# RWKV-7 chunk inverses on 32-wide diagonal tiles, with the decays' affine steps folded away and the normed rows completed later

## The chip, the cores and the metric

The kernel runs on one core of a Trainium2 chip. The metric is device time in microseconds (us), from start to end of one launch. Engines are called as in the profile: PE (TensorE matmul), PEld (its weight load), DVE (VectorE), ACT (ScalarE), POOL (GpSimd), SP (SyncE, which issues most DMAs).

## What is computed

The reference is a whole small network on 256 tokens of width 1024, in float32. A first block of two attention and feed-forward layers ends in an RMS norm. A second block of two layers follows: a layer norm, a hybrid mixer, a residual and layer norm, a mixture of 32 experts, a residual and layer norm. The hybrid mixer has three parts side by side, on one input projection: SSD (512 wide), RWKV-7 (256 wide, 4 heads of 64) and GLA (256 wide). The change touches RWKV-7, whose recurrence per head is

```
w = -softplus(-(w0 + tanh(w_lr) @ w2)) - 0.5;  decay = exp(-exp(w));  a = sigmoid(a0 + a_lr @ a2)
k = k * (1 + (a - 1) * k_a)
sa    = state @ (-kk_t)
state = state * w_t + sa (kk_t * a_t)^T + v_t k_t^T
y_t   = state @ r_t
```

## The kernel before

The kernel does not run the recurrence step by step. It cuts the 256 tokens into two chunks of 128 (NT = 2, index c). Inside a chunk, all `sa` follow from a unit-triangular system of 128 x 128 per head; the kernel forms its inverse `Ti` (4 heads side by side, 128 x 512) and multiplies with it (L1083). Each layer l of the second block calls `ln_T` (norm and transpose of the rows), `mixer` and `moe`, in this order.

**Norm.** `ln_T` leaves the rows `x` centred but not yet scaled. Its inner function `finish` completes them, x = x * r + bias row, with two ACT operations (L791) and two POOL operations (L792) of 128 x 1024. They are needed only at the residual, at the mixer's end. The mixer calls `finish` right after the low-rank projections (L918).

**Decays and rates.** The low-rank projections give `ld` and `av` as a tanh (ACT, L920). Two DVE operations (L931, L932) turn them into log decays and rates with a multiply and an add. Prefix sums over time follow (L937), then `rel` and `ex` (L945, L947), their exponentials (L948 to L950), and `bet`, `alp` (L963 to L966), the factors of the pair matrices (`pairmat`, L981).

**Inverse.** From the pair matrix in PSUM, DVE makes `N` (L994), and `Ti` starts as the part of N next to the diagonal, plus the identity (L995, L996); PE transposes it into `X` (L999). Then six levels double the size of the inverted diagonal blocks. Per level and chunk:

```
M  = N * mask of the level      POOL L1004, 128 x 512
pw = M^T X     (4 heads)        PE L1007, then ACT copy Wm, L1009
px = Ti^T Wm   (levels 1 to 5)  PE L1013, then DVE X += px, L1018
pt = Wm^T Ti                    PE L1016, then DVE Ti += pt, L1019
```

All are full 128 x 128 matrices, though at level lv only blocks of 2^lv are nonzero in what is added. A float32 matmul of this kind has two records in the trace, so one group of 4 heads is 8 records.

**Order.** A scheduler in the framework decides the order on each engine when the program is built; on the chip every engine runs its list in order. Between the groups of the inverse it places whatever else is ready: the projections (helpers at L129, fp32 weights split into two parts by ACT L159 and DVE L161), the other pair matrices (L981), and the block on `w_small` (L1134 to L1165: dt, the GLA gates and their scan). After the inverse come the RWKV output (L1078 to L1120), the rest of the `gv` and `gg` projections (L129), the GLA score matmuls (L1212, 32 x 32 tiles given by `tile_position`), SSD, the out-projection, and the experts. The experts' weights are asked for once a tile of the GLA output exists.

## Time and profile before

| what | us |
|---|---|
| median of 3 runs (1994.29 to 1998.39) | 1995.66 |
| profiled execution, total | 1999.68 |
| its span in the trace | 1998.0 |
| PE busy | 1861.1 (93%) |
| DVE busy | 784.9 (39%) |
| ACT busy | 600.1 (30%) |
| POOL busy | 194.6 (10%) |

The profiled execution's granted TensorE clock is 0.973 on average. The page's slices of 49.95 us show the stages: the first block up to about 606 us, the mixer of layer 0 in slices 13 to 17, its experts up to about 1300 us, the mixer of layer 1 in slices 27 to 31, its experts up to the end. A busy share is an average over all of these, so the mixers have to be read by windows of their own.

### The profile page before, as it was taken

What the parts mean: (1) busy time and instruction counts of PE and PEld (TensorE: products, weight loads), DVE (VectorE), ACT (ScalarE), POOL (GpSimd) and SP (SyncE); (2) the same over time, 40 slices, a digit from 0 to 9 for tenths busy, and PEclk for the clock granted to TensorE, in tenths of its full rate; (3) what the DMA queues carried; (4) which work ended last, traced back from release to release, by engine and by line L of the source; (5) the groups of instructions that cost most, each with busy time, mean ns of one, the idle gap of its engine ahead of it and who ended that gap; (6) DMA issues with size and microseconds to landing.
All of it is one profiled execution on the core that took longest, in us unless ns stands there. A gap on an engine that the chain in (4) does not pass through costs nothing. (4 is left out here: it accounts for less than half of the span.)

```text
span 1998.0 us, 28881 instructions
## 1 busy us (share of the span) xinstructions
PE 1861.1 (93%) x11910; PEld 1285.7 (64%) x11910; DVE 784.9 (39%) x1401; ACT 600.1 (30%) x1002; POOL 194.6 (10%) x321
## 2 busy tenths in 40 slices
PE   8999999999998899899999999879999999999996
PEld 7889998889997788644444333378886444443333
DVE  5654445754447867511111011078574111111012
ACT  5554444654445434211111011153442111111011
POOL 1100000100012423200000000034231000000000
PEclk9899999999999999899999999989998999999998
DMA  6245553345562116699999999841277999999995
GB/s 243 103 154 186 188 198 127 106 158 184 186 251 99 64 65 274 244 385 419 417 418 419 418 418 419 341 141 43 86 295 259 413 418 418 418 418 419 418 418 213
DMA packets 90494, 542.49 MB, mean 272 GB/s; under 512 B 10416, under 2 KB 10928, under 8 KB 38128
## 3 DMA queue, kind: packets, MB, share of 16 engines
q1 hardware_dynamic: 87552, 531.21, 67.8%
q0 software_dynamic: 2512, 9.16, 1.3%
...
HBM read 539.43 MB, written 1.05 MB: 271 GB/s over the span
## 5 line engine op out<-in xcount | busy, mean ns | idle before, releaser
L161 DVE TENSOR_TENSOR hl<-w,hl 128x1024 fp32r<-128x1024 f32 (+2 forms) x252 | 300.2, 1200 | 237.9 <-ACT hl L159 235.4
L159 ACT ACTIVATE hl<-w 128x1024 fp32r<-128x1024 f32 (+2 forms) x252 | 256.6, 1027 | 292.6 <-PE aux L129 113.1
L1726 PE MATMUL aux<-ew_e,XG_e 128*64 128x512 f32 x992 | 253.5, 595 | 7.6 <-DMA ew_e<-in_moe_up 7.5
L1736 DVE SCALAR_TENSOR_TENSOR e_sh_e<-e_sh_e,e_kept_e,aux 128x512 f32<-128x512 f32 x32 | 23.9, 747 | 509.4 <-ACT e_sh_e L1735 496.8
L1726 PEld LDWEIGHTS aux<-ew_e,XG_e 128*64 128x64 f32 x992 | 81.9, 137 | 165.5 <-issue 148.4
L1745 ACT ACTIVATE e_sh_e<-m 128x512 f32<-128x512 f32 x32 | 19.1, 598 | 508.9 <-PE m L1743 508.9
L1726 PE MATMUL aux<-hl,XG_e 128*64 128x512 f32 x480 | 137.8, 606 | 10.1 <-DMA hl<-in_moe_up 6.2
L129 PE MATMUL aux<-hl_f,hl 128*128 128x256 f32 x1056 | 131.4, 284 | 0.6 <-DVE hl_f L245 0.3
L129 PEld LDWEIGHTS aux<-hl_f,hl 128*128 128x128 f32 x1056 | 129.7, 192 | 2.8 <-DVE hl_f L245 0.7
L1726 PE MATMUL aux<-w,XG_e 128*64 128x512 f32 x384 | 126.7, 594 | 5.1 <-DMA w<-in_moe_gate 5.1
L129 PE MATMUL m<-hl_f,hl 128*128 128x256 f32 x1056 | 130.3, 283 | 0.0
L129 PEld LDWEIGHTS m<-hl_f,hl 128*128 128x128 f32 x1056 | 128.3, 192 | 0.0
L1758 DVE TENSOR_TENSOR e_y_e<-m,e_y_e 128x512 fp32r<-128x512 f32 x64 | 44.2, 691 | 213.3 <-ACT e_y_e L1757 213.3
L182 PE MATMUL mm<-hl,m_f 128*128 128x512 f32 x528 | 123.5, 390 | 0.0
L1754 PE MATMUL m<-ew_e,e_sh_e 128*64 128x512 f32 x448 | 115.5, 597 | 0.0
L182 PEld LDWEIGHTS mm<-hl,m_f 128*128 128x128 f32 x528 | 97.9, 188 | 19.4
L1757 ACT ACTIVATE e_y_e<-m 128x512 fp32r<-128x512 f32 x64 | 38.2, 597 | 199.8 <-PE m L1754 199.8
L1726 PEld LDWEIGHTS aux<-hl,XG_e 128*64 128x64 f32 x480 | 41.9, 138 | 82.3 <-issue 52.3
L1650 PE MATMUL m<-e_y_e,e_h_e 128*128 128x256 f32 x256 | 69.2, 308 | 24.1 <-DVE e_y_e L1636 24.1
L129 PE MATMUL aux<-hl_m,hl 128*128 128x256 f32 (+1 forms) x576 | 83.3, 305 | 6.5 <-DVE r_k_m L898 4.9
L1766 PE MATMUL mm<-e_y_e,slots_e 128*128 128x512 f32 x256 | 78.4, 429 | 6.1 <-PEq L1789 4.7
L129 PEld LDWEIGHTS aux<-hl_m,hl 128*128 128x128 f32 (+1 forms) x576 | 77.0, 200 | 9.4 <-DVE r_k_m L898 5.1
(560 smaller groups left out, 2850.2 us busy)
## 6 DMA issues: line engine op xcount, KB each, us to landing
...
```

Source lines behind the costliest of these rows:

```text
L129: self.nc.tensor.matmul(out, x, y, start=(i == 0 and j == 0), stop=(i == n - 1 and j == len(terms) - 1))
L159: nc.scalar.activation(vo(hv), s, AF.Copy)
L161: nc.vector.tensor_tensor(vo(lv), s, vo(hv).bitcast(F32), op=OP.subtract)
L182: self.nc.tensor.matmul(acc[t][h], u1, u2, start=(kg == 0 and q == 0), stop=(kg == n_k - 1 and q == len(terms) - 1))
L1650: nc.tensor.matmul(p[:, j], src[:, t, c], sel[t], start=n == 0, stop=n == 3)
L1726: nc.tensor.matmul(p[64 * i:64 * i + 64], xg[:, 4 * q + kk, o:o + CAP], tiles[nm, q, e](kk), start=(q == 0 and kk == 0), stop=(q == 1 and ...
L1736: i = nc.vector.scalar_tensor_tensor(s_, s_, at[pr][1], up, op0=OP.mult, op1=OP.mult)
L1745: nc.scalar.activation(hh, p, AF.Copy)
L1754: nc.tensor.matmul(p[64 * i:64 * i + 64], hh[:, f, 64 * i:64 * i + 64], tiles["down", hf, es[i]](f), start=f == 0, stop=f == 3)
L1757: nc.scalar.activation(yh, p, AF.Copy)
L1758: nc.vector.tensor_tensor(yl, p, yh.bitcast(F32), op=OP.subtract)
L1766: nc.tensor.matmul(acc[t][hf], sT[:, t * P:(t + 1) * P], ys[:, 2 * hf + q], start=False, stop=pr == last and q == 1)
```

## The change

Four things change in `mixer` and `ln_T`.

1. The inverse works on the four 32 x 32 diagonal blocks of each head for levels 1 to 4, as 32 x 32 matmuls with `tile_position` (32b, 32b); `TX` holds a 32-wide `Ti` and its transpose, which DVE's 32 x 32 block transpose makes from the sum (no `px` step, no PE transposes). One POOL operation per chunk makes all four masked copies `Ml`. Level 5 joins pairs of blocks (32 x 32 tiles off the diagonal), level 6 the two halves (64 x 64 tiles). Ti is zeroed by POOL and filled by copies. The masks lv0 to lv6 are gone, and with them 896 columns of the constants' load.
2. The affine steps on `ld` and `av` are gone; their constants go into the scan, the exponentials' scale and two fused operations.
3. `finish` is four DVE operations of 128 x 512, issued after the last copy of the inverse.
4. The block on `w_small` stands ahead of the inverse in the program.

```diff
-MCONST = (("blk", P), ("gla_mask", 192)) + tuple((f"lv{n}", P) for n in range(7))
+MCONST = (("blk", P), ("gla_mask", 192))
-    early = T([P, 2048], "x_early")
+    early = T([P, 1088], "x_early")
@@ ln_T
     def finish(after):
-        r2 = k.t(W, [P, NT], "ln_r2")
-        for t in range(NT):
-            nc.gpsimd.tensor_copy(r2[:, t:t + 1], after)
-            nc.gpsimd.tensor_copy(r2[:, t:t + 1], rs[t])
-            nc.scalar.activation(x[:, t], x[:, t], AF.Copy, scale=r2[:, t:t + 1])
-            nc.gpsimd.tensor_tensor(x[:, t], x[:, t], rows[1], op=OP.add)
+        for xh, r, h in ((xh, rs[t], h) for t in range(NT) for h, xh in enumerate(row_halves(x)[t])):
+            with k.tc.issue_after(after):
+                nc.vector.scalar_tensor_tensor(xh, xh, r, rows[1][:, h * 512:(h + 1) * 512], op0=OP.mult, op1=OP.add)
 
@@ mixer: decays and rates
-    finish(lr[:, :1])
...
     cd = -0.5 * math.exp(-0.5)
-    nc.vector.tensor_scalar(ld, ld, cd, cd, op0=OP.mult, op1=OP.add)
-    nc.vector.tensor_scalar(av, av, 0.5, 0.5, op0=OP.mult, op1=OP.add)
-
     cum = T([P, 2, S], "r_cum")
     for j in range(2):
         for c in range(NT):
-            nc.vector.tensor_tensor_scan(cum[:, j, tk(c)], k.ones, ld[:, j, tk(c)], 0.0, op0=OP.mult, op1=OP.add)
+            nc.vector.tensor_tensor_scan(cum[:, j, tk(c)], k.ones, ld[:, j, tk(c)], 0.0, op0=OP.add, op1=OP.add)
     cv = cum.rearrange("p j (c t) -> p j c t", c=NT)
     mid, last = cv[:, :, :, 63], cv[:, :, :, P - 1]
     nc.vector.tensor_sub(car, last[:, :, 0], mid[:, :, 0])
     nc.vector.tensor_add(car, car, mid[:, :, 1])
-    nc.scalar.activation(car, car, AF.Exp)
+    nc.scalar.activation(car, car, AF.Exp, scale=cd)
     rel, ex, e_in = (T([P, 2, S], f"r_{n}") for n in ("rel", "ex", "ein"))
     nc.vector.tensor_tensor(rel.rearrange("p j (c t) -> p j c t", c=NT), cv,
                             mid[:, :, :, None].to_broadcast([P, 2, NT, P]), op=OP.subtract)
-    nc.vector.tensor_sub(ex, rel, ld)
-    nc.scalar.activation(e_in, rel, AF.Exp, scale=-1.0)
-    nc.scalar.activation(ex, ex, AF.Exp)
-    nc.scalar.activation(rel, rel, AF.Exp)
+    nc.vector.scalar_tensor_tensor(ex, rel, -1.0, ld, op0=OP.add, op1=OP.subtract)
+    nc.scalar.activation(e_in, rel, AF.Exp, scale=-cd)
+    nc.scalar.activation(ex, ex, AF.Exp, scale=cd)
+    nc.scalar.activation(rel, rel, AF.Exp, scale=cd)
...
     bet = T([P, 2, S], "r_bet")
-    nc.vector.tensor_mul(bet, av, kk_)
-    nc.vector.tensor_mul(bet, bet, e_in)
+    nc.vector.scalar_tensor_tensor(bet, av, 1.0, kk_, op0=OP.add, op1=OP.mult)
+    nc.vector.scalar_tensor_tensor(bet, bet, 0.5, e_in, op0=OP.mult, op1=OP.mult)
...
@@ mixer: the inverses (the block on w_small, dt and the gate scan now stands ahead of this)
+    lvm = const["gla_mask"]
+    Ti = [T([P, 4, P], f"r_T{c}") for c in range(NT)]
+    blk = lambda b: slice(32 * b, 32 * b + 32)
+    up, dn = slice(0, 64), slice(64, P)
+    TX, Ml, M5, M6, X6 = {}, {}, {}, {}, {}
     for c in range(NT):
+        nc.gpsimd.memset(k.late(Ti[c], anchor=r2[:, 0, :1]), 0.0)
+        f1, f2 = (T([P, 512], f"r_{n}{c}") for n in "XN")
+        h4 = lambda x: x.rearrange("p (h t) -> p h t", h=4)
+        X6[c], M5[c], N, M6[c] = h4(f1[:64, :256]), h4(f1[:, 256:384]), h4(f1[:, 384:]), h4(f2[:64, :256])
+        TX[c] = f2[:, 256:].rearrange("p (i h t) -> p i h t", i=2, h=4)
+        nc.gpsimd.memset(k.late(X6[c][blk(0), :, 32:], anchor=r2[:, 0, :1]), 0.0)
         p = pairmat(bet, alz, c)
-        N[c], X[c], Ti[c] = (T([P, 4, P], f"r_{n}{c}") for n in "NXT")
-        nc.vector.tensor_tensor(N[c], p, b4(r2[:, c]), op=OP.mult)
-        nc.vector.tensor_tensor(Ti[c], N[c], mask("lv0"), op=OP.mult)
-        nc.vector.tensor_tensor(Ti[c], Ti[c], k.ident[:, None, :].to_broadcast([P, 4, P]), op=OP.add)
-        p = k.ps([P, 4, P])
+        for b in range(4):
+            nc.vector.tensor_tensor(N[blk(b)], p[blk(b), :, blk(b)], b4(r2[:, c], 32)[blk(b)], op=OP.mult)
+        Ml[c] = T([P, 4, 4, 32], f"r_M{c}")
+        nc.gpsimd.tensor_tensor(Ml[c], N[:, None].to_broadcast([P, 4, 4, 32]),
+                                lvm[:, :4, None].to_broadcast([P, 4, 4, 32]), op=OP.mult)
+        nc.vector.tensor_tensor(TX[c][:, 0], N, lvm[:, 4:5].to_broadcast([P, 4, 32]), op=OP.mult)
+        nc.vector.tensor_tensor(TX[c][:, 0], TX[c][:, 0], lvm[:, 5:6].to_broadcast([P, 4, 32]), op=OP.add)
+        nc.vector.transpose(TX[c][:, 1].rearrange("p h t -> p (h t)"), TX[c][:, 0].rearrange("p h t -> p (h t)"))
+        for b in (0, 2):
+            nc.vector.tensor_tensor(M5[c][blk(b)], p[blk(b), :, blk(b + 1)], b4(r2[:, c], 32)[blk(b)], op=OP.mult)
+        nc.vector.tensor_tensor(M6[c], p[up, :, dn], b4(r2[:, c], 64)[up], op=OP.mult)
+    def tiles32(out, lhs, rhs, rows, cols):
         for h_ in range(4):
-            nc.tensor.transpose(p[:, h_], Ti[c][:, h_], k.ident)
-        nc.scalar.activation(X[c], p, AF.Copy)
-    for lv in range(1, 7):
+            for b, q in zip(rows, cols):
+                nc.tensor.matmul(out[blk(q), h_], lhs(b, h_), rhs(b, h_), start=True, stop=True,
+                                 tile_position=(32 * b, 32 * q))
+    for lv in range(1, 5):
         for c in range(NT):
-            M = T([P, 4, P], "r_M", bufs=4)
-            nc.gpsimd.tensor_tensor(M, N[c], mask(f"lv{lv}"), op=OP.mult)
-            pw = k.ps([P, 4, P])
-            for h_ in range(4):
-                nc.tensor.matmul(pw[:, h_], M[:, h_], X[c][:, h_], start=True, stop=True)
-            Wm = T([P, 4, P], "r_W", bufs=2)
+            t_, x_, M = TX[c][:, 0], TX[c][:, 1], Ml[c][:, 4 - lv]
+            pw = k.ps([P, 4, 32])
+            tiles32(pw, lambda b, h_: M[blk(b), h_], lambda b, h_: x_[blk(b), h_], range(4), range(4))
+            Wm = T([P, 4, 32], "r_W", bufs=2)
             nc.scalar.activation(Wm, pw, AF.Copy)
-            if lv < 6:
-                px = k.ps([P, 4, P])
-                for h_ in range(4):
-                    nc.tensor.matmul(px[:, h_], Ti[c][:, h_], Wm[:, h_], start=True, stop=True)
-            pt = k.ps([P, 4, P])
-            for h_ in range(4):
-                nc.tensor.matmul(pt[:, h_], Wm[:, h_], Ti[c][:, h_], start=True, stop=True)
-            if lv < 6:
-                nc.vector.tensor_add(X[c], X[c], px)
-            nc.vector.tensor_add(Ti[c], Ti[c], pt)
+            p = k.ps([P, 4, 32])
+            tiles32(p, lambda b, h_: Wm[blk(b), h_], lambda b, h_: t_[blk(b), h_], range(4), range(4))
+            nc.vector.tensor_add(t_, t_, p)
+            nc.vector.transpose(x_.rearrange("p h t -> p (h t)"), t_.rearrange("p h t -> p (h t)"))
+    for c in range(NT):
+        for b in (1, 3, 0, 2):
+            nc.scalar.activation(Ti[c][blk(b), :, blk(b)], TX[c][blk(b), 0], AF.Copy)
+        for b in (0, 1):
+            nc.gpsimd.tensor_copy(X6[c][blk(b), :, blk(b)], TX[c][blk(b), 1])
+        t5 = lambda b, h_: TX[c][blk(b), 0, h_]
+        pw = k.ps([P, 4, 32])
+        tiles32(pw, lambda b, h_: M5[c][blk(b), h_], lambda b, h_: TX[c][blk(b), 1, h_], (0, 2), (1, 3))
+        Wm = T([P, 4, 32], "r_W", bufs=2)
+        for b in (1, 3):
+            nc.scalar.activation(Wm[blk(b)], pw[blk(b)], AF.Copy)
+        p = k.ps([P, 2, 4, 32])
+        w5 = lambda b, h_: Wm[blk(b), h_]
+        tiles32(p[:, 1], t5, w5, (1,), (1,))
+        tiles32(p[:, 0], w5, t5, (1, 3), (0, 2))
+        nc.vector.tensor_copy(X6[c][blk(1), :, blk(0)], p[blk(1), 1])
+        nc.scalar.activation(Ti[c][blk(2), :, blk(3)], p[blk(2), 0], AF.Copy)
+        nc.vector.tensor_copy(Ti[c][blk(0), :, blk(1)], p[blk(0), 0])
+    for c in range(NT):
+        pw = k.ps([P, 4, 64])
+        for h_ in range(4):
+            nc.tensor.matmul(pw[dn, h_], M6[c][:, h_], X6[c][:, h_], start=True, stop=True, tile_position=(0, 64))
+        Wm = T([P, 4, 64], "r_W6", bufs=2)
+        nc.scalar.activation(Wm[dn], pw[dn], AF.Copy)
+        p = k.ps([P, 4, 64])
+        for h_ in range(4):
+            nc.tensor.matmul(p[up, h_], Wm[dn, h_], Ti[c][dn, h_, dn], start=True, stop=True, tile_position=(64, 0))
+        i = nc.vector.tensor_copy(Ti[c][up, :, dn], p[up])
+    finish(i.ins)
...
-        nc.vector.tensor_scalar(f, av[:, j], col("k_a", j), oka[:, j:j + 1], op0=OP.mult, op1=OP.add)
+        nc.vector.tensor_scalar(f, av[:, j], hka[:, j:j + 1], oka[:, j:j + 1], op0=OP.mult, op1=OP.add)
```

What this does to the lists shows at three places, all in layer 0. On PE, in the middle of the inverse (`mm` are the inverse's results in PSUM, r_T, r_X, r_W its operands, `m3` other results), before:

```order
L1016 MATMUL mm_534_5981<-r_T0_m0_513_5900,r_W_m0_532_5974 128x128 x4
L1007 MATMUL mm_536_5990<-r_X1_m0_517_5914,r_M_m0_535_5988 128x128 x4
L129 MATMUL m3_601_6246<-r_bs_m0_580_6171,x_early_m0_475_5547 128x512
L1013 MATMUL mm_538_5997<-r_W_m0_537_5995,r_T1_m0_518_5915 128x128 x4
L1016 MATMUL mm_539_6002<-r_T1_m0_518_5915,r_W_m0_537_5995 128x128 x4
L1007 MATMUL mm_541_6011<-r_X0_m0_512_5899,r_M_m0_540_6009 128x128 x4
```

and now, where r_N0 and r_N1 hold TX of the two chunks:

```order
L1052 MATMUL mm_530_6055<-r_N0_m0_517_5940,r_M0_m0_519_5950 32x32 x16
L1131 MATMUL m3_568_6410<-r_rows_m0_563_6396,r_AK0_m0_567_6408 128x64 x3
L977 MATMUL m3_569_6416<-r_alz0_m0_490_5654,r_k_m0_500_5686 128x256
L1052 MATMUL mm_532_6074<-r_N0_m0_517_5940,r_W_m0_531_6072 32x32 x16
L1052 MATMUL mm_533_6093<-r_N1_m0_521_5961,r_M1_m0_523_5971 32x32 x16
L977 MATMUL m3_569_6416<-r_alz1_m0_491_5657,r_k_m0_500_5686 128x256
L1052 MATMUL mm_535_6112<-r_N1_m0_521_5961,r_W_m0_534_6110 32x32 x16
```

Three groups of four full matmuls per level and chunk became two groups of sixteen small ones, with less other work between them.

On DVE, at the decays, before:

```order
L161 TENSOR_TENSOR hl_68<-w_67,hl_68 128x320
L931 TENSOR_SCALAR r_ld_m_484_5633<-r_ld_m_484_5633 128x512
L932 TENSOR_SCALAR r_av_m_485_5634<-r_av_m_485_5634 128x512
L937 SCALAR_TENSOR_TENSOR r_cum_m_496_5678<-const_69,r_ld_m_484_5633 128x128 x4
L941 TENSOR_TENSOR x_small_m_476_5548<-r_cum_m_496_5678 128x2
```

and now (L933 is the scan, L896 a token shift of k):

```order
L896 SCALAR_TENSOR_TENSOR r_k_m_500_5686<-aux_5695,const_69,r_k_m_500_5686 128x255
L161 TENSOR_TENSOR hl_68<-w_67,hl_68 128x320
L896 SCALAR_TENSOR_TENSOR r_k_m_500_5686<-aux_5695,const_69,r_k_m_500_5686 128x255
L933 SCALAR_TENSOR_TENSOR r_cum_m_495_5669<-const_69,r_ld_m_484_5635 128x128 x2
L1100 TENSOR_SCALAR r_f_m_560_6381<-r_av_m_485_5636,x_small_m_476_5548 128x256
L1101 TENSOR_TENSOR r_k_m_500_5686<-r_k_m_500_5686,r_f_m_560_6381 128x256
```

The two operations between the tanh and the scan are gone, and both halves of k's token shift stand ahead of the scan.

On DVE, at the end of the inverse, now:

```order
L1084 COPY r_T1_m0_515_5936<-mm_553_6335 32x4x32
L1095 COPY r_T0_m0_514_5935<-mm_556_6358 64x4x64
L1140 SCALAR_TENSOR_TENSOR r_QB1_m0_580_6452<-m3_579_6449,x_small_m0_476_5548 128x128
L1144 TENSOR_TENSOR r_QK1_m0_582_6460<-m3_581_6457,x_small_m0_476_5548 128x512
L1095 COPY r_T1_m0_515_5936<-mm_559_6371 64x4x64
L789 SCALAR_TENSOR_TENSOR x_1_64<-x_1_64,ln_st_m0_457_5475,row_n_456_5472 128x512 x2
L789 SCALAR_TENSOR_TENSOR x_1_64<-x_1_64,ln_st_m0_458_5476,row_n_456_5472 128x512 x2
L1148 TENSOR_TENSOR r_bo_m0_584_6464<-m3_583_6462,r_v_m0_501_5687 128x512
L1157 TENSOR_TENSOR r_rows_m0_563_6396<-r_rows_m0_563_6396,mm_590_6497 128x256
```

The four operations of `finish` (L789) stand between the inverse's last copy and the first DVE step of the output stage (L1157, before L1080).

## Rows read from the trace of the kernel before

**Rows 1.** The page's part 1: busy time, share and instructions by engine

```profile
PE 1861.1 (93%) x11910; PEld 1285.7 (64%) x11910; DVE 784.9 (39%) x1401; ACT 600.1 (30%) x1002; POOL 194.6 (10%) x321
```

**Rows 2.** The page's part 2: DMA engines' busy tenths and GB/s in 40 slices

```profile
DMA  6245553345562116699999999841277999999995
GB/s 243 103 154 186 188 198 127 106 158 184 186 251 99 64 65 274 244 385 419 417 418 419 418 418 419 341 141 43 86 295 259 413 418 418 418 418 419 418 418 213
```

**Rows 3.** Windows of the two mixers: length, busy time by engine, PEclk, DMA share, GB/s

```profile
637.07:655.63 18.56, 15.45 (x110) 14.08 (x109) 17.17 (x30) 13.13 (x25) 7.35 (x8) 0.92 0.23 67
655.63:719.20 63.57, 56.66 (x431) 52.23 (x428) 49.50 (x75) 20.19 (x36) 27.07 (x24) 0.97 0.16 54
719.20:732.24 13.04, 13.04 (x127) 11.62 (x125) 5.25 (x15) 6.20 (x13) 2.06 (x2) 1.00 0.13 54
...
1325.86:1348.46 22.60, 17.68 (x128) 17.27 (x127) 19.35 (x33) 13.61 (x26) 7.05 (x6) 0.85 0.35 124
1348.46:1407.00 58.54, 54.45 (x428) 50.17 (x427) 45.82 (x74) 20.22 (x36) 25.20 (x24) 1.00 0.12 39
1407.00:1419.90 12.90, 12.89 (x126) 11.58 (x125) 5.44 (x15) 6.26 (x13) 2.06 (x2) 1.00 0.19 75
```

**Rows 4.** Timeline of PE, two groups of the inverse in layer 0, and a later wait

```profile
685.13 1.06 PE L1016 MATMUL mm<-r_T_m,r_W_m 128*128 128x128 f32 x8
686.02 1.06 PE L1007 MATMUL mm<-r_X_m,r_M_m 128*128 128x128 f32 x8
...
707.31 1.16 PE L1013 MATMUL mm<-r_W_m,r_T_m 128*128 128x128 f32 x8 [1.27 <-ACT r_W_m L1009]
```

**Rows 5.** Timeline of PE, layer 0: inverse used, then 96 GLA records

```profile
718.31 1.00 PE L1083 MATMUL mm<-r_rows_m,r_T_m 128*128 128x64 f32 x8
...
732.24 0.33 PE L1212 MATMUL m<-s_G_m,s_G_m 32*32 32x32 f32 x16
...
733.19 1.70 PE L868 MATMUL aux<-hl_m,hl 128*128 128x256 f32 x12
```

**Rows 6.** Timeline of PE: waits and projections ahead of N, both layers

```profile
637.07 10.77 PE L129 MATMUL aux<-hl_m,hl 128*128 128x256 f32 x87
650.62 1.05 PE L973 MATMUL mm<-x_early_m,r_sq_m 128*128 128x2 f32 x8 [2.77 <-ACT r_sq_m L961]
...
1337.60 7.94 PE L129 MATMUL aux<-hl_m,hl 128*128 128x256 f32 x48 [4.92 <-DVE r_k_m L898]
```

**Rows 7.** Timeline of DVE and POOL, layer 0: decays, finish, first N

```profile
637.53 3.30 DVE L931 TENSOR_SCALAR r_ld_m<-r_ld_m 128x512 f32<-128x512 f32 x1 [3.35 <-ACT r_ld_m L920]
640.76 2.62 DVE L932 TENSOR_SCALAR r_av_m<-r_av_m 128x512 f32<-128x512 f32 x1
...
655.63 0.67 DVE L994 TENSOR_TENSOR r_N_m<-mm,x_small_m 128x512 f32<-128x512 f32 x1
...
640.48 2.61 POOL L792 TENSOR_TENSOR x<-x,row_n 128x1024 f32<-128x1024 f32 x1
```

**Rows 8.** Groups of instructions: busy, mean ns, idle before and its releaser

```profile
L1004 POOL TENSOR_TENSOR r_M_m<-r_N_m,x_early_m 128x512 f32<-128x512 f32 x24 | 35.6, 1508 | 24.5 <-ACT r_W_m L1009 14.2 <-DVE r_N_m L994 9.9 <-POOL r_roz_m L1033 0.3
L1019 DVE TENSOR_TENSOR r_T_m<-r_T_m,mm 128x512 f32<-128x512 f32 x24 | 16.4, 684 | 5.9 <-PE mm L1016 5.8
L1009 ACT ACTIVATE r_W_m<-mm 128x512 f32<-128x512 f32 x24 | 14.2, 592 | 40.6 <-PE mm L1007 40.6
L1212 PE MATMUL m<-s_xd_m,s_G_m 32*32 32x32 f32 x384 | 6.5, 193 | 0.0
L995 DVE TENSOR_TENSOR r_T_m<-r_N_m,x_early_m 128x512 f32<-128x512 f32 x4 | 6.3, 1580 | 0.0
L996 DVE TENSOR_TENSOR r_T_m<-r_T_m,const 128x512 f32<-128x512 f32 x4 | 4.8, 1188 | 0.0
L1063 DVE SCALAR_TENSOR_TENSOR r_QB_m<-m,x_small_m 128x128 f32<-128x128 f32 x16 | 4.8, 343 | 2.5 <-PE m L981 2.5
```

**Rows 9.** Timeline of DVE: three operations of the form that finish now uses

```profile
611.78 2.23 DVE L740 SCALAR_TENSOR_TENSOR x<-ln_y_m,ln_st_m,row_n 128x512 f32<-128x512 f32 x3
```

61 lines of the change are left out of this document (30 added, 31 removed).

## The prediction

> **What bounds the kernel now.** I read the shares first: PE is busy 93% of the span, DVE 39% [rows 1]. That is an average over unlike stages. The DMA row splits it: the two long runs of nines are the experts, where the weights' stream sets the pace, and the two dips to ones are the mixers, where it cannot [rows 2]. All of the change lies in the dips (and one constant load). The experts' weights are asked for only after the GLA output, so a mixer that ends earlier moves everything behind it by as much: I count mixer time one for one.
>
> The windows then show who works there [rows 3]. In layer 0, from the first N to the last inverse matmul (63.57 us), PE is busy 56.66 and DVE 49.50. In the 13.04 us after it PE is busy throughout. In layer 1 it is 54.45 of 58.54, then 12.89 of 12.90. So PE's own work sets the pace, DVE is close behind, and a saving on one engine counts only down to the other's work. The timeline says what the PE work is: groups of eight records start 0.89 us apart (685.13 to 686.02), and late in the inverse, where other work has run out, PE waits, 1.27 us for ACT's copy at 707.31 [rows 4]. The inverse is first used at 718.31 and the GLA matmuls begin at 732.24 [rows 5]; I take their start as the end of the stretch, since behind it the order is unchanged. N starts at 655.63 [rows 7], so the stretch to be changed is 76.6 us in layer 0. In layer 1 it is 58.54 + 12.90 = 71.4 [rows 3].
>
> **Inverse, PE.** Per layer 12 groups of L1007, 10 of L1013 and 12 of L1016 go: 34 x 0.89 = 30.3 us, with the two transposes (four records of eight, half a group each) about 31. Added are 8 x 32 + 2 x 20 + 2 x 8 = 312 small matmuls, 624 records if they have two each. The nearest row is L1212, also 32 x 32 by tile position: 96 records in 732.24 to 733.19 [rows 5], 0.95 / 96 = 9.9 ns each, so 6.2 us. One such record alone lasts 193 ns [rows 8], and a group that others wait for shows it once: 26 groups x 0.19 = 4.9. I take 11; the lower end is 6.2, the upper end is 624 x 0.193 = 120, which is rival B. I choose the low end because L1212 is the only row of the same kind of instruction. PE saves 20 us per layer. Its work in the stretch falls from 56.66 + 13.04 = 69.7 to 50, in layer 1 from 54.45 + 12.89 = 67.3 to 47.
>
> **Inverse and finish, DVE.** Per layer L994 (2 x 0.67), L995 (2 x 1.58), L996 (2 x 1.19), and 22 sums of 0.684 (12 of L1019, ten of L1018, same form) go: 1.3 + 3.2 + 2.4 + 15.0 = 21.9 us [rows 7, 8]. Added are 42 small operations: 8 for N, 4 for TX, 10 block transposes, 6 for M5 and M6, 8 sums, 6 copies. They are 128 x 128 or less. The trace has no block transpose. It has a 128 x 128 operation from PSUM at 0.343, the nearest row, and a sum of 128 x 512 at 0.684, the upper end [rows 8]. I take 0.32 each, since many are smaller than 128 x 128: 13.4 us (range 10 to 17, as ten transposes at 0.684 would add 3.6). The finish adds 4 x 0.74 = 3.0 [rows 9]. Net DVE falls from 49.50 + 5.25 = 54.8 [rows 3] to 49.3, as much as PE has left. The finish steps stand ahead of the output stage's first DVE step; DVE is busy only 5.25 of the 13.04 us there [rows 3], and PE has the remaining projections to do meanwhile, so I cost them at nothing beyond their busy time; without that cover they would be 3 us per layer.
>
> **The chain.** Per level it is: a group, ACT copy, a group, DVE sum, DVE transpose. That is 0.35 + 0.4 + 0.35 + 0.32 + 0.32, with four handovers of 0.25 (the idle time ahead of L1019, 5.9 us over 24 [rows 8]): 2.7 us, both chunks side by side. One unrelated DVE operation in the way makes it 3.5. Four levels take 14, the last two together 6, the head (N, TX, one POOL mask at 1.5 [rows 8] beside them) 5.5: Ti after some 26 us, against 62.7 before (655.63 to 718.31). What PE then still has is the output stage and the remaining projections, 17 us: the 13.9 of before [rows 5], and 25 more projection records (77 stand behind the first use of Ti now, 52 before) at 10.77 / 87 = 0.124 [rows 6]. 26 + 17 = 43 is below PE's 50, so PE stays the bound. Before, PE was busy 69.7 of 76.6 (91%) and 67.3 of 71.4 (94%). At 95%, since the chain leaves slack but the fillers are scarcer, the stretch becomes 52.5 in layer 0 and 50 in layer 1: 24.1 and 21.4 us less.
>
> **Decays and rates.** L931 (3.30) and L932 (2.62) go from the path to the scan [rows 7]. Beside them POOL does its step of finish, L792 [rows 7]. In layer 0 the projections cover most of it: L129 runs 10.77 us from 637.07, and PE then waits 2.77 for the squares [rows 6]. I count 2.6. In layer 1 PE waits 4.92 for k's token shift, which stood behind L932 on DVE and now stands ahead of the scan: I count 4.9. What is late next in both is PE's own projections. The POOL and ACT steps of finish leave the front too; nobody waits for them there.
>
> **Smaller parts.** POOL loses 12 masks of 1.5 us per layer and gains two of that size, memsets and small copies; it is not a bound in the stretch (27.07 of 63.57 [rows 3]). The block on w_small only moves: same work, earlier, and the GLA scan with it; its DVE steps now share the head of the inverse, which is in the 3.5 us per level. The constants' load loses 896 columns of 128 rows, 0.46 MB; layer 1's copy falls in the experts' stream of layer 0, 1.1 us at the 418 GB/s there [rows 2]; layer 0's lies where DMA is not full, nothing.
>
> **The sum.** Layer 0: 24.1 + 2.6 = 26.7. Layer 1: 21.4 + 4.9 = 26.3. Load: 1.1. Together 54 us: from the profiled execution's 1999.68 to 1945.6. The median of before is 4 us lower than that execution, and the same step down from 1995.66 gives 1942. The ends: if groups stream at 9.9 ns with nothing around them (4.9 us) and PE has no holes (2.5), each layer gains 34, and 1927 results.
>
> **Rivals.**
>
> *A, the chain becomes the bound.* The fillers between the groups are now few, DVE has 49 us of its own work, and a sum or transpose that queues behind a split of 1.2 us or a GLA operation of 0.7 to 1.8 makes a level 5.5 us. Four levels are then 22, Ti comes after 34, and with 17 behind it and waits in the tail the stretch is about 60: 16 and 11 us gained, plus the front less what PE loses in clock. Where PE waited ahead of N, the granted clock was 0.92 and 0.85, against 0.97 and 1.00 in the stretches behind [rows 3], so part of the time runs at the lower of its two levels, 1.2 instead of 2.4 GHz. I put that at 3 us per layer: 1966, in the worst case 1976. For it speaks that DVE was already busy 49.50 of 63.57 us [rows 3]; against it, that the two chunks remain independent of each other, so one can work while the other waits.
>
> *B, the small tiles do not overlap, and the kernel becomes slower.* All four diagonal tiles of a group use different rows of the array and write one PSUM tile; the L1212 matmuls that I take the price from use one row group per head and differ only in columns. If the records ran one after another at 193 ns [rows 8], a group of 32 records would take 6.2 us, 120 us per layer against 31 removed: 80 to 90 us more per layer, about 2150. The kernel is slower than before from the point where a record costs (27 + 11) / 0.624 = 61 ns, six times the price that I took. For it speaks that no row shows such tiles; against it, that neighbouring records of L1212 overlap in the trace to a twentieth of their length.
>
> The Trainium skill speaks for B: its page "TensorEngine Tiling (Array Packing)", section "Restrictions and Gotchas", says that different row tiles cannot access the same PSUM bank at the same time. No row here shows four row tiles writing to one bank, so the trace neither agrees nor disagrees; by that rule alone the time would be B's, if each tile waits for the one before it to leave the bank, and mine if only the write at the end is shared.
>
> *C, the gain is taken back.* If the experts' stream began at a time set by its queue and not by the mixer, only the load's 1.1 us would stay: 1994.5. The dips in [rows 2] speak against it, since a queue that was free would fill them.
>
> *D, more.* DVE operations at 0.25 instead of 0.32 and streaming groups: 1915 to 1925.
>
> **How the numbers follow.** My forecast (1922 to 1960) has 0.75, A (1960 to 1976) 0.12, D 0.04, B 0.06, C 0.03. The predicted time is 1942. The range 1922 to 1976 takes in A and the lower bound of the unknown costs, and leaves out B, C and most of D, about 0.13. A measurement of this kernel tells some 0.2% (4 us) from no change; faster by more than that are the forecast, A and D, 0.91; the same is C, 0.03; slower is B, 0.06.
>
> **What would show it.** In the changed kernel: sixteen-matmul groups (L1052) of 0.3 to 0.5 us each (over 1.5 means B); the first L1160, which uses Ti, some 26 to 33 us after the first L1036; the GLA matmuls (L1256) 50 to 53 us after it in both layers; PE busy about 50 us in that stretch; no wait of PE for k's shift in layer 1; the transposes (L1065) at 0.25 to 0.45 us; the experts of both layers as long as before. If PE waits for DVE or ACT through the levels with over 8 us of idle time per layer, A holds. I am wrong altogether if the experts' stages change their length, or if the time ahead of N grows.

## The result and the profile after

The changed kernel takes 1938.56 us (median of 4 runs, 1932.54 to 1939.87) against 1996.36 us before (4 runs): a ratio of 0.9705, 95% interval 0.9681 to 0.9728, so 58 us faster. 1942 had been predicted. It was measured once more, beside three other kernels:

> The changed kernel once more, beside the kernels of this group on the same chip, so that small differences can be told: 1938 us, ratio 0.968 to 0.973.

That gave 1941.22 us, ratio 0.9729 (0.9697 to 0.9760). The first profiled execution of the changed kernel has a span of 1938.2 us against 1998.0.

The page's part 1 for the changed kernel shows PE busy 49 us less at the same share, and 688 more PE instructions; compare [rows 1]:

```profile
PE 1811.9 (93%) x12598; PEld 1233.0 (64%) x12598; DVE 756.0 (39%) x1435; ACT 593.1 (31%) x1018; POOL 163.6 (8%) x315
```

Where the time went is read from marks on the timelines: the start of the norm's transposes (PE L260) as start of a mixer, the first operation that makes N (DVE), the first matmul that uses Ti, and the first and last record of the GLA score matmuls. Distances between them, in us, layer 0 / layer 1, worked out from each kernel's timelines:

| kernel | start to N | N to Ti's use | Ti's use to GLA | GLA matmuls | both mixers, start to end of GLA |
|---|---|---|---|---|---|
| before | 42.8 / 45.1 | 62.7 / 57.5 | 13.9 / 14.1 | 19.3 / 19.3 | 274.8 |
| changed | 38.0 / 41.1 | 33.5 / 35.2 | 17.0 / 17.2 | 19.1 / 19.1 | 220.3 |
| changed, again | 38.0 / 40.9 | 33.6 / 34.9 | 17.0 / 17.2 | 19.1 / 19.1 | 220.0 |

The mixers give 54.5 us of the 59.8 between the two spans. The rest of the program, 1723 us before and 1718 now, is not the same in any two profiles here (1714 to 1724 over all of them), so 5 us either way is what one execution differs from another by. That makes the table a finer instrument than the total: two profiles of the changed kernel agree in it to 0.3 us.

Windows of the changed kernel from N to the GLA matmuls (length, busy time of PE, PEld, DVE, ACT, POOL, PEclk, DMA share, GB/s), layer 0 and then layer 1; they answer to [rows 3]:

```profile
646.62:680.17 33.55, 28.25 (x723) 22.35 (x724) 28.84 (x80) 15.75 (x40) 10.96 (x19) 1.00 0.16 60
680.17:697.20 17.03, 16.96 (x159) 15.45 (x157) 11.66 (x26) 7.65 (x16) 4.19 (x4) 1.00 0.12 37
...
1311.52:1323.60 12.08, 8.67 (x210) 7.78 (x208) 10.39 (x33) 6.12 (x11) 5.43 (x11) 1.00 0.17 71
1323.60:1337.50 13.90, 13.90 (x353) 10.85 (x347) 8.94 (x23) 3.57 (x10) 2.04 (x2) 0.51 0.24 79
1337.50:1346.72 9.22, 8.96 (x174) 6.73 (x163) 6.95 (x21) 5.62 (x18) 3.26 (x6) 1.00 0.02 4
1346.72:1363.95 17.23, 17.14 (x160) 15.21 (x158) 12.91 (x26) 7.68 (x16) 3.31 (x4) 1.00 0.18 62
```

In layer 0 the stretch is 50.6 us (predicted 52.5) with PE busy 45.2 of it and DVE 40.5; in layer 1 it is 52.4 (predicted 50), and 13.9 us of that ran at a granted clock of 0.51, the 1.2 GHz level, behind a window in which PE was busy 8.67 of 12.08 us. The timeline of PE shows how a level looks now:

```profile
658.16 0.45 PE L1052 MATMUL mm<-r_N_m,r_W_m 32*32 32x32 f32 x32
658.44 0.48 PE L1052 MATMUL mm<-r_N_m,r_M_m 32*32 32x32 f32 x32
658.85 0.88 PE L1131 MATMUL m<-r_rows_m,r_AK_m 128*128 128x64 f32 x6
...
665.82 0.39 PE L1052 MATMUL mm<-r_N_m,r_M_m 32*32 32x32 f32 x25 [1.26 <-issue]
...
680.17 1.00 PE L1160 MATMUL mm<-r_rows_m,r_T_m 128*128 128x64 f32 x8
...
689.84 7.43 PE L129 MATMUL aux<-hl,hl_m 128*128 128x256 f32 x60
697.20 0.33 PE L1256 MATMUL m<-s_G_m,s_G_m 32*32 32x32 f32 x16
```

A group of 32 records gives way to the next after 0.28 us (658.16 to 658.44), 8.7 ns a record, where a group of before took 0.89 [rows 4]. 77 projection records now stand behind the first use of Ti, 52 before; the last 60 of them run in one piece (7.43 us). The groups of instructions give the new small operations (busy us, mean ns, idle before):

```profile
L1052 PE MATMUL mm<-r_N_m,r_W_m 32*32 32x32 f32 x576 | 10.3, 207 | 0.2 <-ACT r_W_m L1061 0.2
L1065 DVE STREAM_TRANSPOSE r_N_m<-r_N_m 128x128 f32<-128x128 f32 x16 | 4.8, 299 | 0.0
L1036 DVE TENSOR_TENSOR r_X_m<-mm,x_small_m 32x128 f32<-32x128 f32 x16 | 4.5, 283 | 0.2
L1061 ACT ACTIVATE r_W_m<-mm 128x128 f32<-128x128 f32 x16 | 4.4, 277 | 16.6 <-PE mm L1052 16.6
L1064 DVE TENSOR_TENSOR r_N_m<-r_N_m,mm 128x128 f32<-128x128 f32 x16 | 4.4, 276 | 3.2 <-PE mm L1052 3.1
L1040 DVE TENSOR_TENSOR r_N_m<-r_X_m,x_early_m 128x128 f32<-128x128 f32 x4 | 3.3, 818 | 0.0
```

### The profile page after: what moved, and what is told of

Read it like the earlier page. It is cut to its first block, busy times and chain, and to the rows that moved or that the text cites. A ratio compares the mean times of both kernels' runs of the same rounds, so it can differ in the third digit from the quotient of the medians.

```text
span 1938.2 us, 30268 instructions
## 1 busy us (share of the span) xinstructions
PE 1811.9 (93%) x12598; PEld 1233.0 (64%) x12598; DVE 756.0 (39%) x1435; ACT 593.1 (31%) x1018; POOL 163.6 (8%) x315
## 5 line engine op out<-in xcount | busy, mean ns | idle before, releaser
L1787 ACT ACTIVATE e_sh_e<-m 128x512 f32<-128x512 f32 x32 | 19.1, 598 | 505.7 <-PE m L1785 505.7
L1796 PE MATMUL m<-w,e_sh_e 128*64 128x512 f32 x240 | 81.6, 606 | 0.0
L129 PE MATMUL aux<-hl_m,hl 128*128 128x256 f32 (+1 forms) x576 | 77.7, 293 | 1.6 <-ACT hl_m L782 0.8
## 6 DMA issues: line engine op xcount, KB each, us to landing
ew_e<-in_moe_gate SPq DMA_DIRECT2D x62, 1024.0 KB, 16.2
hl<-in_moe_gate SPq DMA_DIRECT2D x60, 512.0 KB, 13.4
```

Of the source, the lines that this page charges most:

```text
L129: self.nc.tensor.matmul(out, x, y, start=(i == 0 and j == 0), stop=(i == n - 1 and j == len(terms) - 1))
L1787: nc.scalar.activation(hh, p, AF.Copy)
L1796: nc.tensor.matmul(p[64 * i:64 * i + 64], hh[:, f, 64 * i:64 * i + 64], tiles["down", hf, es[i]](f), start=f == 0, stop=f == 3)
```

## Experiments: one part undone at a time

The first question is whether the inverse carries the gain. The old inverse in the changed kernel:

```diff
-    lvm = const["gla_mask"]
...
+    N, X, Ti = {}, {}, {}
...
+            i = nc.vector.tensor_add(Ti[c], Ti[c], pt)
     finish(i.ins)
```

> The changed kernel with the inverse of before (128 x 128 matmuls, its masks loaded again); decays, finish and the early gate block stay changed. Theory (the gain is PE work taken out of the inverse): only the gain ahead of N is left, some 5 to 10 us, so about 1988 us (ratio 0.996), and the stretch from the first N to the GLA matmuls is back at 70 to 76 us in both layers. Rival (the gain comes from the front and from the gate block's new place, which feeds PE during the inverse): 1975 us or less (ratio under 0.990).

It took 1988.24 us, ratio 0.9966 (0.9951 to 0.9981). The table's sum is 266.6, 8.2 below before: 5.4 of it ahead of N, the stretch from N to GLA at 74.1 and 71.7. Without the new inverse nearly everything is lost, as the theory said. The opposite, the new inverse alone in the kernel of before:

```diff
-    N, X, Ti = {}, {}, {}
...
+    lvm = const["gla_mask"]
...
+        i = nc.vector.tensor_copy(Ti[c][up, :, dn], p[up])
```

> The kernel of before with the new inverse alone; decays, finish and gate block as before, and the masks' columns still loaded. Theory: nearly the whole stretch gain, 24 + 21 us, so about 1950 us (ratio 0.977). With the other kernel (all but the inverse) the two gains add up to the whole 58 us. Rival (the parts need each other: POOL's finish beside DVE's small operations, no filler for PE): 1960 us or more, and the gains do not add up.

It took 1970.93 us, ratio 0.9903 (0.9870 to 0.9936): the theory's 1950 fell. By the marks the sum is 249.8, a gain of 25.0, and 25.0 + 8.2 = 33.2 is far from 54.5. Yet the inverse itself was as short as in the changed kernel:

| kernel | start to N | N to Ti's use | Ti's use to GLA | GLA matmuls | both mixers |
|---|---|---|---|---|---|
| old inverse | 38.4 / 44.1 | 60.7 / 59.2 | 13.4 / 12.5 | 19.1 / 19.1 | 266.6 |
| new inverse alone | 41.9 / 44.8 | 30.6 / 35.7 | 21.7 / 20.7 | 25.5 / 28.9 | 249.8 |
| old finish | 43.1 / 48.4 | 34.6 / 33.7 | 18.0 / 18.0 | 19.1 / 19.1 | 234.0 |
| old decays | 39.6 / 40.2 | 33.2 / 31.8 | 17.7 / 17.8 | 19.1 / 19.1 | 218.6 |
| late gates | 38.5 / 40.0 | 30.0 / 30.1 | 24.7 / 24.9 | 25.1 / 27.9 | 241.1 |

What it lacks against the changed kernel, 29.5 us, lies in the GLA matmuls (16.2), ahead of N (7.6) and between (5.7). So with the inverse out of the way, PE waited for something else, inside the GLA stage. The waits of PE in the kernel with the new inverse alone, in its GLA stages of layer 0 and layer 1 (us in total, times, longest):

```profile
PE m L1256 <- POOL s_G_m L1235: 5.1, 3, 2.7
...
PE m L1256 <- POOL s_G_m L1235: 6.2, 3, 2.8
```

PE stood idle 4.4 and 5.6 us in these GLA stages (25.52 us with PE busy 21.14, and 28.86 with 23.27), and the rest of the 16.2 went with the clock: granted 0.87 and 0.76 there, 1.00 in the changed kernel. POOL's L1235 makes the GLA factors from the gates' scan. That pointed to the block on `w_small`, whose move I had called free. Put back behind the RWKV output, all else changed:

```diff
-    wsm = k.wload(a["w_small"][l], (KD, 40))
...
-        nc.vector.tensor_tensor_scan(gc[:, sl], k.ones, gu[:, sl], 0.0, op0=OP.mult, op1=OP.add)
...
         nc.vector.tensor_mul(ry, ry, gT)
...
+    wsm = k.wload(a["w_small"][l], (KD, 40))
...
+        nc.vector.tensor_tensor_scan(gc[:, sl], k.ones, gu[:, sl], 0.0, op0=OP.mult, op1=OP.add)
     w = slab(2312, P)
```

> The changed kernel with the block on w_small (dt, GLA gates, their scan) back behind the RWKV output in the program; all else changed. The prediction costed this move at nothing: within 2 us of the changed kernel (ratio 0.970 to 0.972). Rival, from the run with the new inverse alone, where the GLA matmuls began early but then took 25.5 and 28.9 us instead of 19: the GLA factors come late when the inverse is short, PE waits for them between the four groups of GLA matmuls, and 10 to 16 us are lost: about 1952 us (ratio 0.978).

It took 1961.72 us, ratio 0.9847 (0.9823 to 0.9871), some 23 us slower than the changed kernel. The inverse is even shorter (30 us), and it does not help. The waits of PE in the GLA stage of layer 0, and the timelines of PE and DVE:

```profile
PE m L1253 <- POOL s_G_m L1232: 4.7, 2, 3.2
```

```profile
680.25 0.17 DVE L1185 TENSOR_TENSOR x_small_m<-m,x_small_m 128x16 f32<-128x16 f32 x1 [0.38 <-PE m L1184]
...
688.54 0.73 DVE L1206 TENSOR_TENSOR_SCAN g_q_m<-const,g_q_m 128x128 f32<-128x128 f32 x2
```

```profile
698.53 0.33 PE L1253 MATMUL m<-s_G_m,s_G_m 32*32 32x32 f32 x16 [3.21 <-POOL s_G_m L1232]
...
703.15 0.33 PE L1253 MATMUL m<-s_xd_m,s_G_m 32*32 32x32 f32 x16 [1.51 <-POOL s_G_m L1232]
```

The gates' DVE chain starts at 680 and its scan ends at 689, then the factors take DVE and POOL another 10 us, while PE is through with its projections at 695. In the changed kernel the same scan was done at 653. The wait is only half of the price. Windows of the GLA matmuls (columns as above), layer 0 and 1 of this kernel, then layer 0 of the changed one:

```profile
698.53:723.60 25.07, 23.56 (x514) 20.96 (x515) 18.47 (x28) 9.39 (x22) 7.49 (x15) 0.80 0.35 129
1375.18:1403.10 27.92, 27.51 (x514) 24.19 (x515) 19.16 (x27) 9.13 (x22) 6.36 (x14) 0.64 0.33 115
...
697.20:716.30 19.10, 19.10 (x515) 17.20 (x515) 13.49 (x21) 9.11 (x21) 4.71 (x12) 1.00 0.37 137
```

From the first use of Ti to the end of the GLA matmuls PE stood idle for 10.3 us in the two layers, 0.2 in the changed kernel. The same GLA records (514 against 515) then kept PE busy 4.5 and 8.4 us longer, at a granted clock of 0.80 and 0.64: in layer 1 PE hardly waited any more (27.51 of 27.92 us busy), and the stage was still 8.8 us longer. So late factors cost a wait, and behind the wait a stretch at the 1.2 GHz level that cost as much again.

The gates' place is worth 20.8 us in the marks (241.1 against 220.3), and nearly all of the 21.3 by which the kernel with the old inverse (8.2) and the new inverse alone (25.0) together fall short of 54.5. In the kernel of before, where the inverse took long enough to hide the gates, the move was not run alone; with the old inverse and all other parts changed, only 2.8 us were gained behind the start of N.

Next, the norm's completion at its old place and on its old engines:

```diff
-                nc.vector.scalar_tensor_tensor(xh, xh, r, rows[1][:, h * 512:(h + 1) * 512], op0=OP.mult, op1=OP.add)
...
+            nc.scalar.activation(x[:, t], x[:, t], AF.Copy, scale=r2[:, t:t + 1])
+            nc.gpsimd.tensor_tensor(x[:, t], x[:, t], rows[1], op=OP.add)
...
+    finish(lr[:, :1])
...
-    finish(i.ins)
```

> The changed kernel with the norm completed as before (two ACT and two POOL operations right behind the low-rank projections). Theory: 2 to 4 us slower than the changed kernel, about 1941 us (ratio 0.972), because ACT's two operations of 1.15 us come ahead of the tanh that PE waits for, and POOL works beside DVE there. Rival (the four DVE operations behind the inverse hold up the output stage by 3 us per layer): faster than the changed kernel, about 1934 us (ratio 0.969).

It took 1951.13 us, ratio 0.9787 (0.9764 to 0.9810): more than the theory's 2 to 4 us. 12.4 us of the marks' 13.7 lie ahead of N. The timelines of DVE, POOL and ACT at the decays of layer 0 in this kernel:

```profile
629.33 3.05 DVE L937 TENSOR_TENSOR_SCAN r_cum_m<-const,r_ld_m 128x128 f32<-128x128 f32 x2 [2.09 <-ACT r_ld_m L922]
...
633.68 2.93 DVE L937 TENSOR_TENSOR_SCAN r_cum_m<-const,r_ld_m 128x128 f32<-128x128 f32 x2
```

```profile
629.38 2.40 POOL L792 TENSOR_TENSOR x<-x,row_n 128x1024 f32<-128x1024 f32 x1
...
633.54 2.47 POOL L792 TENSOR_TENSOR x<-x,row_n 128x1024 f32<-128x1024 f32 x1
```

```profile
627.79 1.15 ACT L791 ACTIVATE x<-x,ln_r_m 128x1024 f32<-128x1024 f32 x1 [1.22 <-POOL ln_r_m L790]
```

and of DVE and POOL at the same place in the changed kernel:

```profile
629.17 0.73 DVE L933 TENSOR_TENSOR_SCAN r_cum_m<-const,r_ld_m 128x128 f32<-128x128 f32 x2
629.82 2.53 DVE L1100 TENSOR_SCALAR r_f_m<-r_av_m,x_small_m 128x256 f32<-128x256 f32 x1
...
632.80 0.73 DVE L933 TENSOR_TENSOR_SCAN r_cum_m<-const,r_ld_m 128x128 f32<-128x128 f32 x2
```

```profile
629.36 1.01 POOL L814 MEMSET r_alz_m<- 128x512 f32 x2
630.29 1.01 POOL L814 MEMSET r_roz_m<- 128x512 f32 x2
631.23 0.97 POOL L814 MEMSET r_z_m<- 128x1024 f32 x1
```

Each pair of scans takes 3 us and ends 0.6 us after the POOL addition beside it; the same pair takes 0.73 in the changed kernel, where POOL is idle or fills zeros. The first scan also starts later, 22.1 us after the mixer's start against 20.5: ACT's part of finish (1.15 us) stands ahead of the tanh that it waits for. When the second pair ends, 4.5 us are lost, 1.6 of them by this start and the rest beside POOL. The Trainium skill says so too: its page "GPSIMD Engine Reference", section "Key points", has GpSimd share its SBUF interfaces with VectorE, with contention where a VectorE instruction has two SBUF inputs or uses a mode with both ports. These scans have two inputs, and the trace agrees, with 0.73 against 3.05 us. Beside POOL the changed kernel still pays, though elsewhere: L1100 takes 2.53 us beside the zero fills, and 0.41 when it comes again at 635.45. Then the two affine operations put back, with the new finish:

```diff
+    nc.vector.tensor_scalar(ld, ld, cd, cd, op0=OP.mult, op1=OP.add)
+    nc.vector.tensor_scalar(av, av, 0.5, 0.5, op0=OP.mult, op1=OP.add)
...
```

> The changed kernel with the two affine operations on decays and rates put back on DVE. Theory (they stand on the path to the scan and ahead of k's shift): 3 to 8 us slower than the changed kernel, about 1944 us (ratio 0.974). Rival (the projections on PE hide them once POOL's finish step is gone from beside them): within 1 us of the changed kernel, ratio 0.970 to 0.971, each of the two operations at 0.4 to 0.7 us instead of 3.30 and 2.62.

1939.09 us, ratio 0.9729 (0.9703 to 0.9756): within what can be told of the changed kernel, and the marks' sum is 1.7 lower. The rival holds. Timelines of DVE and POOL, layer 0, in this kernel:

```profile
630.56 2.08 DVE L929 TENSOR_SCALAR r_ld_m<-r_ld_m 128x512 f32<-128x512 f32 x1 [1.14 <-ACT r_ld_m L918]
...
633.34 0.40 DVE L930 TENSOR_SCALAR r_av_m<-r_av_m 128x512 f32<-128x512 f32 x1
```

```profile
630.46 1.01 POOL L814 MEMSET r_roz_m<- 128x512 f32 x2
631.39 0.97 POOL L814 MEMSET r_z_m<- 128x1024 f32 x1
```

Alone, such an operation takes 0.40 us; beside POOL's zero fill 2.08; beside POOL's additions it took 3.30 and 2.62 [rows 7]. What I had charged to the decays was the price of whatever DVE happens to do while POOL works.

A kernel meant to tell the place of finish from its engines, ACT and POOL operations written behind the inverse:

```diff
-                nc.vector.scalar_tensor_tensor(xh, xh, r, rows[1][:, h * 512:(h + 1) * 512], op0=OP.mult, op1=OP.add)
+                nc.scalar.activation(x[:, t], x[:, t], AF.Copy, scale=rs[t])
+                nc.gpsimd.tensor_tensor(x[:, t], x[:, t], rows[1], op=OP.add)
```

> The changed kernel with the norm completed at the new place (behind the last copy of the inverse) but on the old engines: two ACT operations of 128 x 1024 and two POOL additions. Theory from the run with the old finish (POOL's addition beside the decays stretched two scans from 0.73 to 3.05 and 2.93 us): it is the place that costs, not the engines; behind the inverse few DVE steps stand on the path, so within 4 us of the changed kernel, and the DVE operations beside POOL's additions last longer there. Rival (the engines matter wherever they stand): 8 to 12 us slower, as with the old finish.

1944.15 us, ratio 0.9753 (0.9725 to 0.9781). It did not test the place it was written for: the scheduler put the operations at the front of the mixer, POOL's timeline of layer 0 shows them beside the transposes:

```profile
611.09 2.37 POOL L789 TENSOR_TENSOR x<-x,row_n 128x1024 f32<-128x1024 f32 x1 [0.31 <-ACT x L788]
...
618.73 2.81 POOL L789 TENSOR_TENSOR x<-x,row_n 128x1024 f32<-128x1024 f32 x1 [4.79 <-ACT x L788]
```

There, 10 us ahead of the scans, they cost layer 0 nothing (start to N 38.0, as in the changed kernel); layer 1 lost 5.0 ahead of N, where DVE waited 5.89 us for ACT's half of k (L895) and 2.11 in the changed kernel; why it came later I did not follow further. So the old engines were harmless at the front in layer 0 and not in layer 1; behind the inverse they were not tried. The kernel answers another question: without the four DVE operations behind the inverse, the way from Ti's use to GLA is 16.9 and 17.4 us, against 17.0 and 17.2 with them, so there they cost nothing.

## Experiments: what bounds the stretch now

The small matmuls issued tile by tile instead of round the four diagonal tiles:

```diff
-        for h_ in range(4):
-            for b, q in zip(rows, cols):
+        for b, q in zip(rows, cols):
+            for h_ in range(4):
```

> The changed kernel with the small matmuls of a group issued tile by tile (four heads on one 32 x 32 tile, then the next tile) instead of going round the four diagonal tiles. Same matmuls, same results. If neighbours overlap because they sit on different tiles, a group of 32 records takes 0.8 us or more instead of 0.28, 22 groups per layer, and the kernel is 20 to 40 us slower (ratio 0.98 to 0.99). If the records are issue-bound (8.6 ns each) whichever tile they use, the time stays within 2 us (ratio 0.970 to 0.972). If row tiles that share a PSUM bank hinder each other, this order is faster, groups under 0.25 us.

1972.58 us, ratio 0.9887 (0.9858 to 0.9916), 32 to 36 us slower than the changed kernel by the ratios (0.9729 and 0.9705). PE's timeline at full clock, and the windows of layer 0's inverse up to 690 us:

```profile
653.70 0.87 PE L1052 MATMUL mm<-r_N_m,r_M_m 32*32 32x32 f32 x32 [1.58 <-DVE x_small_m L1009]
654.50 0.74 PE L129 MATMUL aux<-hl_m,hl 128*128 128x256 f32 x4
```

```profile
651.00:661.60 10.60, 9.02 (x133) 8.33 (x131) 10.00 (x27) 5.72 (x10) 4.68 (x6) 0.84 0.01 2
661.60:676.00 14.40, 14.40 (x278) 12.44 (x277) 7.01 (x16) 2.12 (x6) 2.04 (x3) 0.56 0.23 76
676.00:690.00 14.00, 14.00 (x215) 10.59 (x214) 5.52 (x17) 5.62 (x17) 2.64 (x5) 0.50 0.01 2
```

A group goes from 0.38 us (651.83 to 652.21 for the same group in the changed kernel) to 0.80. So records overlap where neighbours sit on different tiles, although all four tiles write the same PSUM tile. The Trainium skill's page "TensorEngine Tiling (Array Packing)", section "Restrictions and Gotchas", has it that different row tiles cannot access one PSUM bank at the same time; here the order that goes round the row tiles is the faster one, 8.7 ns a record, so no price of that rule shows for these 32-column matmuls, and the measurement decides. The doubled group explains only some 8 us per layer (592 records at 0.42 / 32 more each) of the 19 to 23 lost from N to GLA. The rest came with the clock, which fell to 0.56 and 0.50 (the 1.2 GHz level) and was 0.61 on the mean from N to Ti's use. In the window of the fall PE had been idle 1.58 of 10.60 us; after it, PE was busy all the time and the clock stayed low.

Every small matmul twice:

```diff
-        for h_ in range(4):
+        for h_ in [0, 1, 2, 3] * 2:
```

> The changed kernel with every 32 x 32 matmul of the inverse issued twice (the second writes the same result again): 592 more records per layer, 5.1 us of PE at 8.6 ns each. Theory (PE's own work bounds the stretch): 8 to 11 us slower than the changed kernel, about 1948 us (ratio 0.976). Rival (the handovers between DVE, ACT and PE bound the levels, PE waits in them): the extra records fall into the waits, at most 4 us slower, ratio up to 0.973.

1972.12 us, ratio 0.9914 (0.9887 to 0.9942): three to four times what 592 more records per layer cost at 8.6 ns each (5.1 us). N to Ti's use is 47.0 and 46.9, 13 and 12 us more. The window of layer 0, and a gap in a group:

```profile
657.65:670.00 12.35, 10.04 (x401) 8.66 (x400) 7.21 (x17) 3.80 (x9) 2.07 (x2) 0.53 0.26 89
...
670.00:678.00 8.00, 5.23 (x323) 4.28 (x326) 5.45 (x11) 2.41 (x7) 6.03 (x8) 0.88 0.01 4
```

```profile
663.62 0.65 PE L1052 MATMUL mm<-r_N_m,r_W_m 32*32 32x32 f32 x33 [2.31 <-issue]
```

PE gets the clock at 0.53 (the 1.2 GHz level) again, and stops three times in layer 0 inside groups for 5.0 us in all, released by no engine that the profile shows. The DMA queues show what went on: in the gap before 663.62 one 16 KB packet of the queue that the page calls `instruction` moved (661.3 to 662.2). Its row in the view of 661.2 to 662.4, and the rows of that queue on the pages of the changed kernel and of this one:

```profile
q8 instruction: 1, 0.02, 4.7%
...
q8 instruction: 103, 1.69, 0.4%
...
q8 instruction: 113, 1.85, 0.4%
```

The doubled matmuls brought ten more packets. In all kernels here, the 25 gaps of this kind (released by `issue`, over 0.3 us, within the inverses) end 1.2 to 1.6 us after such a packet has landed; the two kernels with the old inverse have none, nor have three with the new one. So PE most likely ran out of instructions and waited for the next ones; that is read from the times, and no run varied it. The changed kernel has two such gaps, 1.26 and 1.04 us, both in layer 0. So PE's path does bound the stretch, but its price is not the records alone.

Each block transpose behind a level's sum twice:

```diff
             nc.vector.transpose(x_.rearrange("p h t -> p (h t)"), t_.rearrange("p h t -> p (h t)"))
+            nc.vector.transpose(x_.rearrange("p h t -> p (h t)"), t_.rearrange("p h t -> p (h t)"))
```

> The changed kernel with each of the eight block transposes per layer behind a level's sum done twice: 2.4 us more DVE work per layer, on the path from one level to the next. Theory (PE's work bounds the stretch): within 2 us of the changed kernel, ratio 0.970 to 0.972. Rival (DVE's own work or its place in the chain bounds the levels): 4 to 6 us slower, about 1943 us (ratio 0.973 to 0.974).

1938.03 us, ratio 0.9727 (0.9713 to 0.9741): as the changed kernel. DVE's 2.4 us more per layer cost nothing that the total shows; N to Ti's use is 33.7 and 36.2 against 33.5 and 35.2. In the changed kernel DVE is already busy 28.84 of 33.55 us there, and still is not the bound. The two kernels differ in more than the transposes, since the scheduler orders every kernel anew. From N to GLA this one takes 48.8 and 49.6 us, less than the 50.6 and 52.4 of the changed kernel. In layer 0 the two gaps (2.3 us together) are missing, and without them 48.8 stands against 48.3; in layer 1 the clock was 0.95 from N to Ti's use, against 0.81. So in layer 0 the 2.4 us cost some 0.5.

Two kernels tried to beat the changed one. The gate block between the making of N and the levels:

```diff
-    wsm = k.wload(a["w_small"][l], (KD, 40))
...
     lvm = const["gla_mask"]
...
+    wsm = k.wload(a["w_small"][l], (KD, 40))
...
     for lv in range(1, 5):
```

> The changed kernel with the gate block placed between the making of N and the levels, instead of ahead of N. Theory (the block must come before the inverse's end, or the GLA factors are late; but its 24 matmuls, 2.9 us, need not stand ahead of N): N starts 2 to 3 us earlier per layer and the GLA matmuls are as dense as in the changed kernel (19 us), so 2 to 6 us faster, ratio 0.967 to 0.970. Rival (the factors are late as soon as the block moves at all): slower by 5 us or more.

1938.30 us, ratio 0.9728 (0.9702 to 0.9755). And, on top of it, POOL's mask operation in two, the larger part behind the transpose:

```diff
+        nc.gpsimd.tensor_tensor(Ml[c][:, 3], N, lvm[:, 3:4].to_broadcast([P, 4, 32]), op=OP.mult)
...
+        with k.tc.issue_after(tr.ins):
+            nc.gpsimd.tensor_tensor(Ml[c][:, :3], N[:, None].to_broadcast([P, 3, 4, 32]),
```

> As the kernel with the gates behind N, and POOL's mask operation in two: the first level's mask alone first (128 x 128), the other three behind the DVE transpose, so that POOL no longer works beside the two DVE operations that took 0.82 us instead of 0.27 on the mean. Theory (POOL work beside DVE costs the head of the inverse 1 us per chunk): another 2 to 4 us faster than the kernel with the gates behind N alone, ratio 0.965 to 0.969. Rival (later masks make the second level wait, or the head is not on the path): no faster than that kernel.

1940.24 us, ratio 0.9730 (0.9704 to 0.9757). Neither differs from the changed kernel measured beside them (0.9729), so the gains that both theories gave did not come, nor did the loss of the first one's rival; the marks' sums are 220.2 and 217.4 against 220.0. N did not start earlier in layer 0 (38.0 in both), where DVE was busy for the 8 us ahead of it (timeline of the first of them), and started 1.8 and 1.6 us earlier in layer 1 (40.9 in the changed kernel); the 3 us of the second kernel are below what the total can tell. The granted clock from N to Ti's use in layer 0 was 0.85 in the first of them, and 1.00 in the changed kernel, so part of any gain there is a matter of the clock.

## Why the prediction was right, and where its steps were not

**The total** was right: 54 us foreseen, 58 measured by the medians, 54.5 by the marks. Layer 0 gave 31.1 (26.7 predicted), layer 1 23.4 (26.3); that the sum came closer than its two halves is luck.

**The stretch** from N to the GLA matmuls was right within 2.5 us per layer (50.6 and 52.4 against 52.5 and 50), and PE's list is its bound, as forecast: doubling DVE's transposes cost next to nothing, more PE work cost at once. Some of its terms were off in directions that cancelled, which is luck too. PE's work in layer 0 was 45.2 us, not 50: the records go by at 8.7 ns instead of 9.9, a group shows no latency of 0.19 when another follows, and the gates' matmuls had left the stretch. DVE had 40.5 us, not 49.3; most of its small operations last 0.276 to 0.299, not 0.32 (L1040, beside POOL's mask, 0.818), and part of its other work had moved ahead of N. PE was busy 89% of the stretch, not 95%: it stood idle 5.4 us, of which 2.7 were waits for DVE at the first level and 2.3 the two gaps in which it most likely waited for its next instructions.

**The chain** was not 26 us long: Ti was used 33.5 and 35.2 us after N. The head was right (5.2 us to the first group, 5.5 predicted). The four levels took 19.5 us in layer 0, not 14, and the last two 8.8, not 6, with the other work of PE's list between the groups. The sum did not suffer, because PE was busy 28.25 of the 33.55 us and had only the forecast 17 left.

**Rival A** (the chain bounds) did not come, but its warning about the clock did in layer 1: 13.9 us at 0.51, after PE had waited 3.4 us in two pieces for the first transposes. The same steps (658.44 to 671.32 in layer 0, 1323.18 to 1338.67 in layer 1) took 12.9 and 15.5 us. But PE stood still 2.3 us of the 12.9, in the two gaps, and 0.15 of the 15.5, so the lower level cost its work 4.8 us, where I had put down 3; the gaps that layer 1 was spared hid half of that.

**Rival B** (tiles do not overlap) was rejected by the changed kernel's own rows: 0.28 us for a group against 6.2.

**The front** was right in size and wrong in cause. I foresaw 2.6 and 4.9 us; 4.8 and 4.0 were measured. I gave them to the two affine operations, whose rows of 3.30 and 2.62 us I took for work. They were 0.40 us of work each and the wait for POOL; put back, they cost nothing that can be told. The gain belongs to finish leaving POOL and ACT (put back, it cost 12.4 us ahead of N), of which I had written that nobody waits for it there. I had the row that said otherwise: POOL's addition stood beside them [rows 7], and a 128 x 512 operation with one input lasted five times as long as a sum with two [rows 8].

**The gate block** was the step that failed worst: "same work, earlier" at no price. Its place was worth 20.8 us. My sum still came out, because I had assumed the order of the changed kernel, in which the GLA stage stays at 19 us; what I did not see is that without this move, much of the time saved in the inverse would have come back, half as PE's wait for the GLA factors and half as the lower clock behind that wait. "Where a stall goes, what is late next" was asked of the front and not of the stretch's end.

**The load** of 1.1 us cannot be seen: the rest of the program differs by up to 10 us between profiles.

What stays open: what makes PE's next instructions late in some inverses and not in others; why layer 1 of the changed kernel fell to the lower clock and layer 0 did not; and why finish on its old engines, at the mixer's front, cost layer 1 five microseconds.
